# Sums made in place in four tiles of the second feed-forward, and a shorter, reordered opening, in a streaming-encoder layer on one core

## The chip, the core and the metric

The kernel runs on one core of one Trainium2 chip. Times are device microseconds of one launch. The core's engines run side by side and each takes its instructions in the order in which they were written to it: PE does matmuls (PEld is its weight load), ACT (ScalarE) and DVE (VectorE) do elementwise work, POOL does little here, and SP issues most of the DMAs. An engine waits on semaphores for what the others make.

## The reference, cut to what matters

One encoder layer in float32 on 256 tokens of width 2048, with a gated feed-forward (inner width 5632) at its beginning and at its end:

```
x = x + 0.5 * swiglu(rms_norm(x, ffn1_norm), ffn1_w_up, ffn1_w_down)
...                       # gated recurrences, then attention over 256 memory tokens
x = x + 0.5 * swiglu(rms_norm(x, ffn2_norm), ffn2_w_up, ffn2_w_down)
return rms_norm(x, final_norm)

def swiglu(h, w_up, w_down):
    gate, up = split(h @ w_up, 2)
    return (silu(gate) * up) @ w_down
```

The change touches the last feed-forward (ffn2) and the first few microseconds of the first (ffn1).

## The kernel before

**Three products for one.** PE multiplies rounded float32 numbers. Each weight tile of 128 x 2048 is loaded into a buffer called `raw`; ACT makes `h`, its rounded copy, and DVE makes `l` = raw - h. The activations are split in the same way into `xh` and `xl`. A product is then h by xh, h by xl and l by xh. `split` (L155) issues the two instructions of a split: ACT at L156, DVE at L157.

**Kinds of tiles.** `plan_ffn` (L166) lists the weight tiles of a feed-forward and gives each a kind; `prepare` (L278) issues its load, sums and splits; `ffn` (L613) issues its matmuls. A "plain" tile gives eight products. A "fast" tile gives seven products of sums of its quarters (as in Strassen's scheme), and needs a second tile `td` with four such sums, 512 columns each: DVE makes the first two with one instruction (L317), the third at L319 and the fourth at L320. Its own last 1536 columns are split into `h` and `l`, and `td` in two halves of 1024 into `th` and `tl`. A "ready" tile finds its four sums in memory, made and stored earlier in the launch, so that `td` is a load (L309) and not work for DVE.

**The second feed-forward.** It has eleven groups of 512 columns, `wu2[g, p]` with eight tiles p in the order 1, 3, 4, 0, 2, 5, 6, 7, and between the groups tiles of the down projection, `wd2`, which work on the turned results of earlier groups (`hidop`). Which tiles are "ready" is said by `sums_ready` (L88); what is left "fast" is: in group 1 tile 6, in group 2 tile 6, in group 3 tiles 5 and 7, in later groups three or four. Tile p of group g is called "tile g.p" below, and t1_7 is the stored sums of tile 1.7.

**What sets the order.** `weights` (L238) prepares two tiles ahead of the one that PE multiplies. A scheduler lays the instructions of each engine in an order, and the pools set the waits: a load waits until the buffer that it overwrites has had its last reader. In ffn2 `raw_tile` (L261) gives out five buffers of 8 KB a partition in a fixed rotation, three from the pool `raw` and then two from `raw2`; a tile and its `td` take one each. Three `h` buffers hold `h` and `th`. The pool `slots` has 22 buffers of 4 KB a partition. SP issues its loads strictly in its list's order, so a load that waits for its buffer holds back those behind it.

**The opening.** `head_x` (L740) loads the block p of the activations (`xf`), `operand_pairs` (L530) scales it by the norm's gains into `xg` (two ACT instructions at L537) and splits it into `xh` and `xl`. Block 0 is made otherwise (`rounded`, `remainder`, L732 and L735); it is scaled into `xg` only for the sums of activations that later tiles need. Nine matmuls on a tile of ones (L143), two passes each, run on PE before its first product.

Of the kernel before, what the change touches and what calls it, by code (L numbers as in the profile page):

```python
# [10 lines left out]
ACT = mybir.ActivationFunctionType  # L11
ALU = mybir.AluOpType

P = 128
T = 256
# [79 lines left out]
def block_kernel(ctx: ExitStack, tc: tile.TileContext, xT, xin, memT, vec, gfin, bgate, lruw, wu1, wd1, win, wv,  # L95
# [15 lines left out]
    scoped = {}  # L111
# [27 lines left out]
    ones = const.tile([P, P], F32, name="ones")  # L139
    dve.memset(ones, 1.0)  # L140
    warm = bank("warm")
    for _ in range(9):
        pe.matmul(warm[:, :P], ones, ones, start=True, stop=True)  # L143
    eps = const.tile([P, 1], F32, name="eps")
    act.activation(eps, ones[:, :1], ACT.Copy, scale=EPS)
# [20 lines left out]
    def plan_ffn(name, wu, wd):  # L166
        for e in orders[name]:
            src = wd[e[4], e[3]] if e[0] == "down" else wu[e[1], e[2]]
            kind = "fast" if e[0] == "fast" else "added" if name == "ffn1" and e[0] == "mixed" and f"M{e[2]}" in FIRST[e[1]] else "plain"
            if e[0] == "down" and 0 < e[4] < NG - 1 and e[4] % 2 == 0 and e[3] % 2:  # L170
                kind = "added"
            if adds(name, e):
                kind = "fast added"
            if sums_ready(name, e):
                kind = "ready"
                t = kept.tile([P, 2048], F32, name=f"t{e[1]}_{e[2]}")
                made_ahead.append((src, t))
                src = src, t
            plan.append(((name,) + e, src, kind))
# [98 lines left out]
    def prepare(src, kind, cuts=1):  # L278

        if kind == "added":  # L280
            raw, l = begun.pop(0)
            h = hp.tile([P, 2048], F32R, name="h", tag="h")
            done["high"] = act.activation(h, raw, ACT.Copy).ins
            return h, l
        raw = raw_tile()
        n = 2048 // cuts
        if kind == "plain":
            h, l = split_tiles()
            for a in range(0, 2048, n):
                first = opening and len(pairs1) == 1 and cuts > 1  # L290
                quarter = src.rearrange("p (a n) -> (p a) n", n=n)[a // n * P:][:P] if cuts > 1 else src
                sp.dma_start(raw[:, a:a + n], quarter)
                if first and not a:
                    dve.tensor_scalar(out=h[:, :n], in0=raw[:, :n], scalar1=1.0, scalar2=None, op0=ALU.mult)
                    remainder(0)
                    done["low"] = dve.tensor_tensor(out=l[:, :n], in0=raw[:, :n], in1=h[:, :n].bitcast(F32),
                                                    op=ALU.subtract).ins
                else:
                    split(h[:, a:a + n], l[:, a:a + n], raw[:, a:a + n])
                if first and a == n:  # L300
                    sp.dma_start(opening[0][:, 272:], block(272, 256))
                    rounded(1)
                    remainder(1)
            return h, l
        if kind == "ready":
            src, t = src
            sp.dma_start(raw[:, 512:], src[:, 512:])
            td = raw_tile()
            sp.dma_start(td, t)  # L309
        else:  # L310
            sp.dma_start(raw, src)
            if "raw2" in scoped:
                td = raw_tile()
            else:
                td = scoped["wide"].tile([P, 2048], F32, name="td", tag="wide")
            two = [v[:, a:a + 1024].rearrange("p (i n) -> p i n", i=2) for v, a in ((td, 0), (raw, 512))]
            dve.tensor_tensor(out=two[0], in0=raw[:, None, :512].broadcast_to([P, 2, 512]), in1=two[1],  # L317
                              op=ALU.subtract)
            dve.tensor_tensor(out=td[:, 1024:1536], in0=raw[:, 1024:1536], in1=td[:, :512], op=ALU.subtract)  # L319
            dve.tensor_tensor(out=td[:, 1536:], in0=raw[:, 1536:], in1=td[:, 1024:1536], op=ALU.subtract)  # L320
        h, l = split_tiles()
        if kind != "fast added":
            split(h[:, 512:], l[:, 512:], raw[:, 512:])
        else:
            act.activation(l[:, 512:], raw[:, 512:], ACT.Copy, scale=-1.0)
            nc.gpsimd.dma_start(l[:, 512:], src[:, 512:], accum_op=ALU.add)
            done["high"] = act.activation(h[:, 512:], raw[:, 512:], ACT.Copy).ins
        th = hp.tile([P, 2048], F32R, name="h", tag="h")
        if "wide" in scoped:
            tl = scoped["wide"].tile([P, 2048], F32R, name="tl", tag="wide")  # L330
        else:
            tl = lp.tile([P, 2048], F32R, name="tl", tag="l")
        for a in (0, 1024):
            split(th[:, a:a + 1024], tl[:, a:a + 1024], td[:, a:a + 1024])
        return (h, l), (th, tl)

    def product(xs, *ws, late=()):
# [189 lines left out]
    BOTH = [0, 2, 4, 6]  # L527
    xd = []

    def operand_pairs(src, gain, q, xg, out, every=False, made=None):  # L530


        for a in src:
            i = len(out)
            g = xg[:, i * 512:(i + 1) * 512]
            for z in range(2):
                act.activation(g[:, z * T:][:, :T], a[:, z * T:(z + 1) * T], ACT.Copy,  # L537
                               scale=gain(4 * q + 2 * i + z))
            if made:
                h, l = made  # L540
            else:
                h, l = slot(F32R, "xh"), slot(F32R, "xl")
                split(h[:, :512], l[:, :512], g)
            less = None if i else (h[:, 512:768], l[:, 512:768])
            if every:
                less = None
                if q == 3:
                    if not i:
                        xd.append(slot(F32R, "xd"))
                    less = [xd[-1][:, a:a + 256] for a in (512 * i, 512 * i + 256)]  # L550
            elif 2 * q + i in BOTH:
                n = 512 * (BOTH.index(2 * q + i) % 2)
                if not n:
                    xd.append(scoped["xd"].tile([P, 1024], F32R, name="xd", tag="xd"))
                less = [xd[-1][:, a:a + 256] for a in (n, n + 256)]
            out.append(((h, l), less))

        def sums(which=((0, "less"), (0, "sums"), (1, "less"), (1, "sums"))):
            s = slot(name="xs")
            for i, ((h, l), less) in enumerate(out):  # L560
                a = [xg[:, i * 512 + j * P:][:, :P] for j in range(4)]

                def made(h, l, n, at, terms):
                    o = [s[:, at + j * P:][:, :P] for j in range(n)]
                    for j, (x, y, op) in enumerate(terms(o)):
                        dve.tensor_tensor(out=o[j], in0=x, in1=y, op=op)
                    split(h, l, s[:, at:at + n * P])

                if less and (i, "less") in which:
                    made(*less, 2, 0, lambda o: ((a[0], a[1], ALU.subtract), (a[2], a[3], ALU.subtract)))  # L570
                if (every or i or 2 * q in BOTH) and (i, "sums") in which:
                    if not every and not i and len(which) > 1:
                        s = slot(name="xs")
                    made(h[:, 512:], l[:, 512:], 4, 512 * i,
                         lambda o: ((a[1], a[3], ALU.add), (o[0], a[0], ALU.subtract),
                                    (a[1], a[0], ALU.subtract), (a[2], o[1], ALU.subtract)))

        return sums
# [161 lines left out]
    def head_x(p):  # L740

        q = p // 2
        if p % 2 == 0:
            xq[q] = slot(name="xf"), slot(name="xg"), []
        src, xg, out = xq[q]
        a = p % 2 * 512
        if p == 0:
            opening.append(slot(name="xf")[:, :528])
            sp.dma_start(opening[0][:, :272], block(0, 272))
            opening.extend((slot(F32R, "xh"), slot(F32R, "xl")))  # L750
            rounded(0)
            sums = None
            pairs1.append(((opening[1], opening[2]), None))
            return
        sp.dma_start(src[:, a:a + 512], block(16 + p * 512, 512))
        if p == 1:
            operand_pairs([opening[0][:, 16:]], gain1, 0, xg, out, made=opening[1:])
            pairs1[0] = out[-1]
        if p == 6:
            sp.dma_start(vt[:, :small_n], vec[:, :small_n])  # L760
        sums = operand_pairs([src[:, a:a + 512]], gain1, q, xg, out)
        if p % 2:
            sums1.append(sums)
        pairs1.append(out[-1])
# [683 lines left out]
```

## Time and profile before

| | |
|---|---|
| median of three runs | 2412.63 us (2412.18 to 2413.09) |
| the profiled execution | 2412.53 us |
| its span in the profile | 2410.8 us |
| PE busy | 2399.4 us (100%) |
| DVE, ACT busy | 2048.3 us (85%), 1466.6 us (61%) |
| granted TensorE clock | 0.999 |
| second feed-forward | about 1740 us to the end |

The profiled execution is 1.7 us longer than its span and 0.1 us under the median. In the views below a row of the timeline has the start in us, the length in us, the engine, the line, the operation, what it writes and reads, how many such instructions run one behind the other, and in brackets the idle time ahead of it with what ended it.

### The profile page before, as it was taken

Reading aid. Unit: us, or ns where it says so; the run is one execution under the profiler, and the core shown is the slowest. Engines: PE = TensorE matmul, PEld = TensorE weight load, DVE = VectorE, ACT = ScalarE, POOL = GpSimd, SP = SyncE. Lnnn points to the kernel's source line nnn. Section 1 sums busy time; section 2 is a strip of 40 time slices with the busy share of each in tenths; the row PEclk is TensorE's granted clock in tenths of the full one; section 3 lists DMA queues with packets and bytes.
Section 4 is the critical chain, followed back from the end, with each engine's and each line's share of the span. In section 5 each row is a group of like instructions: output and inputs, shape, how many; then the busy total and the mean of one; then the engine's idle time right before and its main releaser. Section 6 shows DMA issues by size and latency. Waiting matters only on the chain.

```text
span 2410.8 us, 30823 instructions
## 1 busy us (share of the span) xinstructions
PE 2399.4 (100%) x12102; PEld 2004.9 (83%) x12102; DVE 2048.3 (85%) x2292; ACT 1466.6 (61%) x1502; POOL 101.3 (4%) x164
## 2 busy tenths in 40 slices
PE   9999999999999999999999999999999999999998
PEld 8888888888888888888888888888888888888887
DVE  7999999999866878679786777777799999999995
ACT  8567777777654454476434555545676666666664
POOL 0000000000000000000000000000000000000000
PEclk9999999999999999999999999999999999999999
DMA  8578999999858776769989899876688877787873
GB/s 316 195 233 255 276 276 278 275 275 273 267 216 303 290 265 264 285 263 342 347 339 336 315 343 338 324 290 234 247 312 323 301 273 284 269 294 273 292 279 145
DMA packets 102098, 681.45 MB, mean 283 GB/s; under 512 B 11328, under 2 KB 11840, under 8 KB 29248
## 3 DMA queue, kind: packets, MB, share of 16 engines
q1 hardware_dynamic: 78912, 519.04, 57.4%
q0 software_dynamic: 23040, 160.44, 22.3%
q8 instruction: 95, 1.56, 0.2%
q14 instruction: 51, 0.42, 0.0%
HBM read 617.57 MB, written 61.87 MB: 282 GB/s over the span
## 4 chain that ended last, share of the span: by engine, by line
PE 97%; DVE 1%; DMA 1%; ACT 1%; issue 0%; SPq 0%; ACTq 0%
PE acc L596 36%; PE acc L598 18%; PE acc L345 11%; PE acc L370 8%; PE acc L371 8%; PE acc L373 8%; PE acc L348 6%; PE acc L636 1%; PE acc L513 1%; DMA raw<-wu 1%; DVE tl L157 0%; DVE l L157 0%; PE acc L962 0%; ACT h L156 0%; PE acc L1261 0%
## 5 line engine op out<-in xcount | busy, mean ns | idle before, releaser
L156 ACT ACTIVATE h<-raw 128x2048 fp32r<-128x2048 f32 (+3 forms) x577 | 868.0, 1528 | 643.6 <-PE acc L371 201.4
L157 DVE TENSOR_TENSOR l<-raw,h 128x2048 fp32r<-128x2048 f32 (+2 forms) x405 | 832.8, 2059 | 233.3 <-ACT h L156 230.4
L596 PE MATMUL acc<-h,xh 128*128 128x512 f32 x1220 | 476.0, 392 | 2.4 <-ACT h L156 2.4
L596 PE MATMUL acc<-h,xl 128*128 128x512 f32 x1220 | 473.6, 390 | 0.0
L596 PE MATMUL acc<-h,hidop 128*128 128x512 f32 x1408 | 352.3, 391 | 0.2 <-ACT h L156 0.2
L370 PE MATMUL acc<-h,ops 128*128 128x512 f32 x832 | 326.8, 393 | 0.0
L371 PE MATMUL acc<-h,ops 128*128 128x512 f32 x832 | 324.6, 390 | 0.0
L596 PEld LDWEIGHTS acc<-h,hidop 128*128 128x128 f32 x1408 | 262.8, 188 | 54.1 <-ACT h L156 0.6
L345 PE MATMUL acc<-ops,h 128*128 128x512 f32 x1152 | 277.6, 393 | 0.0
L596 PEld LDWEIGHTS acc<-h,xh 128*128 128x128 f32 x1220 | 229.1, 188 | 55.5 <-ACT h L156 7.7
L596 PEld LDWEIGHTS acc<-h,xl 128*128 128x128 f32 x1220 | 229.3, 188 | 46.3 <-DVE xl L157 0.2
L345 PEld LDWEIGHTS acc<-ops,h 128*128 128x128 f32 x1152 | 211.6, 188 | 41.1
L157 DVE TENSOR_TENSOR tl<-raw,h 128x1024 fp32r<-128x1024 f32 x172 | 203.4, 1218 | 12.4 <-ACT h L156 11.9
L373 PE MATMUL acc<-l,ops 128*128 128x512 f32 x832 | 206.2, 390 | 0.0
L156 ACT ACTIVATE h<-td 128x1024 fp32r<-128x1024 f32 x140 | 146.6, 1055 | 82.1 <-DVE td L317 31.2
L598 PE MATMUL acc<-l,hidop 128*128 128x512 f32 x704 | 190.9, 390 | 0.0
L370 PEld LDWEIGHTS acc<-h,ops 128*128 128x128 f32 x832 | 156.3, 188 | 32.2
L373 PEld LDWEIGHTS acc<-l,ops 128*128 128x128 f32 x832 | 156.2, 188 | 32.3
L371 PEld LDWEIGHTS acc<-h,ops 128*128 128x128 f32 x832 | 156.5, 188 | 31.2
L598 PE MATMUL acc<-tl,xh 128*128 128x512 f32 x624 | 177.6, 392 | 0.0
L157 DVE TENSOR_TENSOR tl<-td,h 128x1024 fp32r<-128x1024 f32 x140 | 169.8, 1217 | 8.3 <-ACT h L156 7.5
L598 PE MATMUL acc<-l,xh 128*128 128x512 f32 x600 | 165.7, 390 | 0.0
(262 smaller groups left out, 2490.7 us busy)
## 6 DMA issues: line engine op xcount, KB each, us to landing
raw<-wu SPq DMA_DIRECT2D x115, 1024.0 KB, 6.6
raw<-wd SPq DMA_DIRECT2D x88, 1024.0 KB, 6.5
prep<-wu POOLq DMA_DIRECT2D x57, 1024.0 KB, 6.9
t<-prep POOLq DMA_DIRECT2D x57, 1024.0 KB, 6.0
raw<-t SPq DMA_DIRECT2D x57, 1024.0 KB, 6.9
raw<-wu SPq DMA_DIRECT2D x57, 768.0 KB, 4.7
raw<-win SPq DMA_DIRECT2D x40, 1024.0 KB, 5.0
raw<-wg SPq DMA_DIRECT2D x32, 1024.0 KB, 6.0
```

Source lines behind the costliest of these rows:

```text
L156: done["high"] = act.activation(h, raw, ACT.Copy).ins
L157: done["low"] = dve.tensor_tensor(out=l, in0=raw, in1=h.bitcast(F32), op=ALU.subtract).ins
L345: pe.matmul(acc, h[:, k * P:(k + 1) * P], xs[k], start=k == 0, stop=False)
L348: done["product"] = pe.matmul(acc[:, :T], l[:, k * P:(k + 1) * P], xs[k][:, :T], start=False, stop=k == KT - 1).ins
L370: pe.matmul(accs[t], x[:, t * P:][:, :P], h[j], start=first and j == 0, stop=False)
L371: pe.matmul(accs[t], x[:, T + t * P:][:, :P], h[j], start=False, stop=False)
L373: done["product"] = pe.matmul(accs[t], x[:, t * P:][:, :P], l[j], start=False, stop=last and j == 3).ins
L513: pe.transpose(acc[:, z * T + t * P:][:, :P], tile[:, t * 512 + (2 * y + z) * P:][:, :P], ident)
L596: pe.matmul(acc, a, b, start=start, stop=False)
L598: pe.matmul(acc, ah, bl, start=False, stop=stop)
L636: pe.transpose(acc[:, z * T + t * P:][:, :P], hid[t][:, (2 * y + z) * P:][:, :P], ident)
```

## The change

**The four tiles of ffn2.** Fast tiles of groups below 4 get the kind "fast early". Their `td` is a buffer of the pool `slots` with the first two sums only. The third sum overwrites the first 512 columns of `raw`, which nothing reads any more, and the fourth the second 512 columns, after these were split: so L320 is issued behind the split. `th` and `tl` of the second half are made from `raw`. Such a tile takes one buffer of the rotation and not two, and keeps it until its second half is split. The rotation stands one place further after these four tiles in all that follows.

**The opening.** Eight warming matmuls instead of nine. The scaling of block 0 into `xg`, which stood ahead of the scaling of block 1, is issued with block 2, behind its split.

```
-    for _ in range(9):
+    for _ in range(8):
         pe.matmul(warm[:, :P], ones, ones, start=True, stop=True)
...
+            if name == "ffn2" and kind == "fast" and e[1] < 4:
+                kind = "fast early"
             if sums_ready(name, e):
                 kind = "ready"
...
             sp.dma_start(raw, src)
-            if "raw2" in scoped:
+            early = kind == "fast early"
+            if early:
+                td = slot(name="td")
+            elif "raw2" in scoped:
                 td = raw_tile()
...
+            third, fourth = (raw[:, :512], raw[:, 512:1024]) if early else (td[:, 1024:1536], td[:, 1536:])
...
-            dve.tensor_tensor(out=td[:, 1024:1536], in0=raw[:, 1024:1536], in1=td[:, :512], op=ALU.subtract)
-            dve.tensor_tensor(out=td[:, 1536:], in0=raw[:, 1536:], in1=td[:, 1024:1536], op=ALU.subtract)
+            dve.tensor_tensor(out=third, in0=raw[:, 1024:1536], in1=td[:, :512], op=ALU.subtract)
+            if not early:
+                dve.tensor_tensor(out=fourth, in0=raw[:, 1536:], in1=third, op=ALU.subtract)
         h, l = split_tiles()
...
+        halves = [td[:, a:a + 1024] for a in ((0,) if kind == "fast early" else (0, 1024))]
+        if kind == "fast early":
+            dve.tensor_tensor(out=fourth, in0=raw[:, 1536:], in1=third, op=ALU.subtract)
+            halves.append(raw[:, :1024])
...
+    def scaled(g, a, gain, k):
+        for z in range(2):
+            act.activation(g[:, z * T:][:, :T], a[:, z * T:(z + 1) * T], ACT.Copy, scale=gain(k + z))
...
             if made:
                 h, l = made
             else:
+                scaled(g, a, gain, 4 * q + 2 * i)
                 h, l = slot(F32R, "xh"), slot(F32R, "xl")
...
         sums = operand_pairs([src[:, a:a + 512]], gain1, q, xg, out)
+        if p == 2:
+            scaled(xq[0][1], opening[0][:, 16:], gain1, 0)
```

The first place is ACT in the opening, from the last two quarters of the first weight tile on. Before:

```order
L156 ACTIVATE h<-raw 128x512 x2
L537 ACTIVATE xg<-xf 128x256 x4
L156 ACTIVATE xh<-xg 128x512
L156 ACTIVATE h<-raw 128x512 x4
L537 ACTIVATE xg<-xf 128x256 x2
L156 ACTIVATE xh<-xg 128x512
L156 ACTIVATE h<-raw 128x512 x4
L537 ACTIVATE xg<-xf 128x256 x2
L156 ACTIVATE xh<-xg 128x512
```

And with the change:

```order
L156 ACTIVATE h<-raw 128x512 x2
L543 ACTIVATE xg<-xf 128x256 x2
L156 ACTIVATE xh<-xg 128x512
L156 ACTIVATE h<-raw 128x512 x4
L543 ACTIVATE xg<-xf 128x256 x2
L156 ACTIVATE xh<-xg 128x512
L543 ACTIVATE xg<-xf 128x256 x2
L156 ACTIVATE h<-raw 128x512 x4
L543 ACTIVATE xg<-xf 128x256 x2
L156 ACTIVATE xh<-xg 128x512
```

The four scalings (blocks 0 and 1) are two (block 1) now, and the two of block 0 stand between block 2's split and the weight tile that goes with block 2.

The second place is SP at the end of group 1: the load of tile 1.6 (the one at L311, or L313 with the change), and what is issued behind it, with the names' numbers. Before:

```order
L311 DMA raw_14684<-wu2 128x2048
L309 DMA raw_14723<-t1_7_111 128x2048
L307 DMA raw2_14721<-wu2 128x1536
L292 DMA raw_14756<-wd2 128x2048
L292 DMA raw_14797<-wd2 128x2048
```

And with the change:

```order
L313 DMA raw_14683<-wu2 128x2048
L309 DMA raw2_14720<-wu2 128x1536
L311 DMA raw2_14722<-t1_7_110 128x2048
L294 DMA raw_14755<-wd2 128x2048
L294 DMA raw_14796<-wd2 128x2048
```

Tile 1.7 (`wu2 128x1536`) is loaded ahead of its stored sums instead of behind them, and since tile 1.6 takes no second buffer, each of the four loads takes the buffer one place earlier in the rotation. Group 2 ends in the same way.

The third place is ACT at the end of group 5, which stands for groups 4 to 10; here `raw_16401` (before) and `raw_16400` are tile 5.7, `raw_16403` and `raw_16402` are its `td`, and the 128x2048 tiles are two of the down projection. Before:

```order
L156 ACTIVATE h_16407<-raw_16401 128x1536
L156 ACTIVATE h_16411<-raw_16403 128x1024
L156 ACTIVATE h_16439<-raw_16438 128x2048
L156 ACTIVATE h_16411<-raw_16403 128x1024
L683 ACTIVATE hid_16465<-acc_16194 128x512
L156 ACTIVATE h_16480<-raw2_16479 128x2048
```

And with the change:

```order
L156 ACTIVATE h_16406<-raw_16400 128x1536
L156 ACTIVATE h_16410<-raw_16402 128x1024
L156 ACTIVATE h_16438<-raw2_16437 128x2048
L156 ACTIVATE h_16479<-raw2_16478 128x2048
L156 ACTIVATE h_16410<-raw_16402 128x1024
L696 ACTIVATE hid_16464<-acc_16193 128x512
```

Though no operation of these groups is changed, the second half of `th` now stands behind both down tiles on ACT, where it stood between them. DVE's `l` of the second down tile moves ahead of that half's `tl` likewise; PE does five matmuls of the first down tile ahead of this half, where it did three; and SP issues the two down loads in the order in which they are needed, where the second went first.

More of the change, by code (lines that the diff above doesn't have):

```diff
@@ L332, in prepare @@
             tl = lp.tile([P, 2048], F32R, name="tl", tag="l")
-        for a in (0, 1024):
-            split(th[:, a:a + 1024], tl[:, a:a + 1024], td[:, a:a + 1024])
+        for a, t in zip((0, 1024), halves):
+            split(th[:, a:a + 1024], tl[:, a:a + 1024], t)
         return (h, l), (th, tl)
@@ L535, in operand_pairs @@
             g = xg[:, i * 512:(i + 1) * 512]
-            for z in range(2):
-                act.activation(g[:, z * T:][:, :T], a[:, z * T:(z + 1) * T], ACT.Copy,
-                               scale=gain(4 * q + 2 * i + z))
             if made:
```

## The prediction

> **What bounds the kernel now.** I read the page's busy shares and its chain first, then what PE waits for in the second feed-forward, then the timelines around the longest of these waits, and the opening.
>
> ```profile
> span 2410.8 us, 30823 instructions
> PE 2399.4 (100%) x12102; PEld 2004.9 (83%) x12102; DVE 2048.3 (85%) x2292; ACT 1466.6 (61%) x1502; POOL 101.3 (4%) x164
> PE 97%; DVE 1%; DMA 1%; ACT 1%; issue 0%; SPq 0%; ACTq 0%
> PE acc L596 <- ACT h L156: 2.3, 3, 1.2
> ```
>
> PE is the bound, and the change takes one short warming matmul from it and no product. It can only gain where PE waits. The last line is PE's waits from 1740 us on (total, times, longest): three waits for ACT's `h`, 2.3 us in all. That is the prize in the second feed-forward; the rest is what reordering costs.
>
> **Group 1.** PE, ACT, DVE and SP around the first wait, PE around the second, the landing of tile 2.7 (size, us from issue to landing), and DMA traffic in the stretch before (last columns: clock, DMA share, GB/s):
>
> ```profile
> 1800.37 0.39 PE L598 MATMUL acc<-l,xh 128*128 128x512 f32 x1
> 1801.66 0.50 PE L596 MATMUL acc<-h,xh 128*128 128x512 f32 x1 [0.90 <-ACT h L156]
> 1795.32 1.06 ACT L156 ACTIVATE h<-raw 128x1024 fp32r<-128x1024 f32 x1 [0.72 <-DVE raw L317]
> 1799.17 4.33 ACT L156 ACTIVATE h<-raw 128x1536 fp32r<-128x1536 f32 x4 [2.79 <-DMA raw<-wu]
> 1798.53 0.68 DVE L320 TENSOR_TENSOR raw<-raw,raw 128x512 f32<-128x512 f32 x1
> 1784.85 1.75 DVE L157 TENSOR_TENSOR l<-raw,h 128x1536 fp32r<-128x1536 f32 x1
> 1786.52 2.35 DVE L157 TENSOR_TENSOR tl<-raw,h 128x1024 fp32r<-128x1024 f32 x2
> 1790.59 0.33 SPq L309 DMA_DIRECT2D raw<-t  x1
> 1790.96 0.43 SPq L307 DMA_DIRECT2D raw<-wu  x1
> 1790.96 8.11 DMA raw<-wu
> 1851.68 0.61 PE L598 MATMUL acc<-l,xh 128*128 128x512 f32 x2
> 1853.47 0.50 PE L596 MATMUL acc<-h,xh 128*128 128x512 f32 x1 [1.18 <-ACT h L156]
> 1849.37 0.68 DVE L320 TENSOR_TENSOR raw<-raw 128x512 f32<-128x512 f32 x1
> 1842.28 0.42 SPq L307 DMA_DIRECT2D raw<-wu  x1
> raw<-wu SPq DMA_DIRECT2D x1, 768.0 KB, 8.6
> 1780.00:1800.00 20.00, 20.00 (x90) 16.58 (x89) 18.07 (x15) 12.17 (x11) 0.00 (x0) 1.00 0.90 331
> ```
>
> ACT's row of four begins with tile 1.7's `h`, which lands at 1799.07 (1790.96 + 8.11), and only then comes the second half of tile 1.6's `th`. That half's last sum ended at 1799.21 (1798.53 + 0.68), so it could have been done from about 1799.24 to 1800.30 (1.06, as for the first half). Instead it ends 1.33 us later, and PE starts at 1801.66 where 1800.60 was due (1800.37 and one matmul's 0.23, the distance of matmuls in a running row). Lost are 1.06 and 0.11 (the first matmul after a stop takes 0.50 and not 0.39): **1.17 us**. Why it lands late: its load takes a buffer behind the stored sums, which SP issued at 1790.59.
>
> With the change tile 1.7 goes ahead of these sums and takes the buffer that the `l` at 1784.85 leaves at 1786.60; the sums take that of the `tl` pair, free at 1788.87. Issued 4.36 earlier, with the same 8.11 it lands at 1794.7, and ACT has done its `h` while DVE makes the third and fourth sum. Those stay as they were (the same three instructions with the same shapes in the same order on DVE; what they write is another buffer, so I take them at their old lengths, and at 0.1 us more or less for the range). So the half is ready at about 1800.30. PE now does one `l` matmul less ahead of it, and wants it at 1800.37. What is late next is therefore the fourth sum itself, 0.07 us short of costing. I take the whole **-1.17**. The 4 KB buffer of `td` I take as free in time: 22 are in turn, and those of the operands that it follows were last read in earlier stages. No row of before shows such a wait; if the buffer were late, DVE's first sum would be, and the half by as much, up to the loss of the 1.17 and no gain beyond it.
>
> **Group 2** is the same place one group on. Tile 2.7 was issued at 1842.28 and took 8.6, to 1850.88, while the fourth sum ended at 1850.05. PE resumed at 1853.47 where 1852.13 was due: 1.34 and 0.11, **-1.45**. Here the half can be ready at 1851.13 against 1851.68, with 0.5 us to spare; the profile names PE for ACT's idle time there, but the landing is what fits. Group 3 has no such wait, and its loads go out earlier: nothing.
>
> *A rule weighed.* The first term rests on ACT not stepping round a tile that has not landed: the row shows 2.79 us idle and then the tile's `h` first. The Trainium skill, Perfetto Trace Analysis, section on the tensor engine's instruction, says the same: ACT and DVE are strict FIFO. By that rule all of 1.17 is SP's order; with a queue that let the ready half pass, before would have no wait and this term would be nothing.
>
> **Groups 4 to 10** keep their operations, but the rotation shifts, and the order around each group's end with it. Group 5 and group 6 before:
>
> ```profile
> 2030.58 0.86 PE L596 MATMUL acc<-h,hidop 128*128 128x512 f32 x3
> 2031.30 0.50 PE L596 MATMUL acc<-h,xh 128*128 128x512 f32 x1
> 2028.31 0.39 PE L596 MATMUL acc<-h,xl 128*128 128x512 f32 x1
> 2028.39 2.86 ACT L156 ACTIVATE h<-raw 128x2048 fp32r<-128x2048 f32 x2 [2.45 <-DMA raw<-wd]
> 2031.63 1.91 ACT L156 ACTIVATE h<-raw 128x2048 fp32r<-128x2048 f32 x1
> raw<-wd SPq DMA_DIRECT2D x1, 1024.0 KB, 4.9
> raw<-wd SPq DMA_DIRECT2D x1, 1024.0 KB, 6.9
> raw<-wd SPq DMA_DIRECT2D x1, 1024.0 KB, 8.3
> 2091.90 0.96 PE L596 MATMUL acc<-h,hidop 128*128 128x512 f32 x3 [0.19 <-ACT h L156]
> 2082.37 7.45 DMA raw<-wd
> ```
>
> Before, ACT waited until 2028.39 for the down tile that was needed first but loaded second (issue to landing 6.9; its neighbours 4.9 and 8.3). Now that tile is loaded first and the other one second, at the time at which the second load went before: it lands at about 2028.3. Its `h` needs the `h` buffer of tile 5.7, which PE reads last at 2028.31 to 2028.70. So ACT: 2028.70 and 1.91 give about 2030.55 (neighbours overlap by 0.1), and 1.06 for the half: 2031.6. PE wants it after five `hidop` matmuls in place of three: 2030.58 + 5 x 0.23 = 2031.7. It just holds, with 0.1 us. In group 6 the load at 2082.37 landed at 2089.83, PE lost 0.35 + 0.11 + 0.15 + 0.11 there (starts of 2091.90 and of the matmuls behind it against steps of 0.23): 0.7. Now that wait goes, but the half comes at about 2092.7, when PE wants it. Between a gain of 0.7 and, in each of seven groups, a wait of 0.1 with a restart of 0.11 (+1.5) I take **-0.4**, nearer to the gain, since group 5's own rows come out on the good side.
>
> **Opening.** ACT, PE and DVE, and the load of block 1:
>
> ```profile
> 3.54 0.43 SPq L755 DMA_DIRECT2D xf<-xT  x1
> xf<-xT SPq DMA_DIRECT2D x1, 256.0 KB, 5.2
> 8.18 1.69 ACT L537 ACTIVATE xg<-xf 128x256 f32<-128x256 f32 x4
> 10.45 2.18 ACT L156 ACTIVATE h<-raw 128x512 fp32r<-128x512 f32 x4
> 11.12 0.51 PE L596 MATMUL acc<-h,xh 128*128 128x512 f32 x1 [0.29 <-ACT h L156]
> 17.00 0.63 ACT L156 ACTIVATE xh<-xg 128x512 fp32r<-128x512 f32 x1
> 17.67 0.69 DVE L157 TENSOR_TENSOR xl<-xg,xh 128x512 fp32r<-128x512 f32 x1 [0.45 <-ACT xh L156]
> 23.05 0.63 ACT L156 ACTIVATE xh<-xs 128x512 fp32r<-128x512 f32 x1 [1.43 <-DVE xs L566]
> 31.20 1.90 ACT L156 ACTIVATE h<-raw 128x2048 fp32r<-128x2048 f32 x1
> 33.16 0.50 PE L596 MATMUL acc<-h,xh 128*128 128x512 f32 x1
> ```
>
> PE waits at 11.12 for the `h` that stands behind all four scalings. Two of them (0.84) move. But block 1 was issued at 3.54 and took 5.2: it lands at about 8.75, and ACT can't begin its scalings before 8.8. They began at about 9.0 (8.18 and half of 1.69). So only 0.2 of the 0.84 is won: 10.92 for 11.12, **-0.20**. The warming matmul less (two of 18 passes of 0.21, 0.4) adds nothing: the first products can start that much earlier, and PE then waits that much longer for this same `h`. Were this cover gone, it would be another -0.4.
>
> Then the price: block 2's `xh` done, two scalings (0.85) go ahead of block 2's weights and block 3. Block 3's `xh` starts at about 17.65, not 17.00: 0.85 later, less the 0.2 won. DVE waits for just that `xh` (0.45 idle), ACT at 23.05 for DVE's sums (1.43 idle), so the delay travels round; I find no slack in between until ACT's `h` at 31.20, whose end at 33.10 PE takes up at 33.16. Block 4's product can take 0.6 of it unharmed; block 5's starts at about 33.8 for 33.16. Block 6's has 1 us. So PE at block 5 is **0.65 later** than before, which includes the 0.20 won (it is waited away).
>
> **Sum**, against the profiled 2412.53: -1.17 - 1.45 - 0.4 + 0.65 = -2.37, so 2410.2. That execution lies 0.1 under the median of the runs, which changes nothing at this precision.
>
> **Rivals.**
>
> 1. *The opening gains.* For it: the scalings are on PE's path at 11.12, and 0.2 to 0.9 lie there. Against: the 31.20 row, where PE has 0.05 of slack. With -0.3 in place of +0.65, 2410.2 becomes 2409.2; with all of 0.84 won, 2408.7.
>
> 2. *Bandwidth (partly hidden).* The 20 us before the first wait moved 331 GB/s at a share of 0.90. If earlier issue only lengthens the transfers, tile 1.7 still goes ahead of 1 MB of sums in SP's order, which is worth some 2 us of landing (6.4 to 8.1 per load, two on the way); it would have to land after 1798 to cost. Then half of both waits remains: 2411.5. The Trainium skill, DMA: Bandwidth & Descriptors, section Specifications, gives about 358 GB/s of HBM per core as the limit; the trace's 331 lies 8% under it and agrees, so by that page little is gained from issuing earlier, and this rival would be the case, at 2411.5.
>
> 3. *Slower: the end of groups 4 to 10.* The second `th` half now stands behind the second down tile on ACT, and the `l`s on DVE likewise. That tile lands at 2028.3, and ACT takes it up at 2028.7. If it landed as late as the third load did (8.3 in place of 6.9, 1.4 later), the half would be 1.0 us late beyond the 0.4 and 0.1 of margin, PE would stop for that and 0.11, and seven groups would cost 7 to 8 us: 2410.6 without the -0.4, so about 2418. It decides from half a us of lateness of that load on, and passes 0.2% from 1.4 us. For it: the margin is thin everywhere. Against: SP issues in order, and the second load's place in time is unchanged. A mild form, 0.2 a group, gives 2412.0.
>
> 4. *The change doesn't do what it says.* Only four tiles are early; were tile 1.7 and 2.7's buffers not free sooner, only the opening's +0.65 would show: 2413.2. The rows at 1784.85 and 1786.52 speak against it.
>
> **How the numbers follow.** My sum 0.50, opening gains 0.12, bandwidth or mild lateness (2411.5 to 2412) 0.22, nothing but the opening 0.08, seven late groups 0.05, other gains beyond 0.2% 0.03. A measurement of this kernel can tell about 0.2%, 4.8 us, from no change: none but the third rival in full and an unseen gain pass that. The range takes in the first two rivals, the mild form of the third and a tenth or two on each side: 2408.5 to 2412.6.
>
> **What would show it.** PE without a wait at 1800 and 1852, tile 1.7 landing by 1796 and 2.7 by 1848; the first product of block 1 at 10.9 and that of block 5 at 33.8; at group ends PE's step from `hidop` to `h` within 0.1 of 0.23. I am wrong if ACT waits for tile 1.7 as before, if PE's waits for `h` from 1950 on exceed 1 us in all, or if block 5's product comes no later than before.

## The result, and the profile after

The changed kernel takes 2416.36 us (median of 22 runs, 2412.57 to 2418.18) against 2412.53 us (22 runs, 2410.53 to 2415.61): the ratio is 1.0014, with a 95% interval from 1.0008 to 1.0020. It is slower by some 3.5 us (3.8 between the medians), where 2.4 us less were forecast. That is under the 0.2% named in the prediction, and the single runs of the two kernels overlap, but the interval lies above 1. The profiled execution took 2415.37 us, 1.0 under the median, with a span of 2413.5, 2.7 longer than before.

The page's span, PE's busy time and the chain's shares, and PE's waits from 1740 us on (total, times, longest):

```profile
span 2413.5 us, 30820 instructions
PE 2400.3 (99%) x12100; PEld 2002.4 (83%) x12100; DVE 2049.5 (85%) x2292; ACT 1467.7 (61%) x1502; POOL 101.6 (4%) x164
PE 93%; DMA 3%; ACT 2%; DVE 2%; issue 1%; SPq 0%; ACTq 0%; DVEq 0%
PE acc L609 <- ACT h L156: 3.8, 6, 1.1
```

PE is as busy as before, but its share of the chain fell from 97% to 93%, and its waits for `h` went from 2.3 us in three to 3.8 in six. They are not the same waits. Here are SP, ACT, DVE and PE where the first one was, in the order of the forecast's steps:

```profile
1786.61 0.33 SPq L309 DMA_DIRECT2D raw<-wu  x1
1796.75 1.49 ACT L156 ACTIVATE h<-raw 128x1536 fp32r<-128x1536 f32 x1 [0.75 <-PE acc L609]
1798.04 0.68 DVE L337 TENSOR_TENSOR raw<-raw 128x512 f32<-128x512 f32 x1
1798.76 4.78 ACT L156 ACTIVATE h<-raw 128x1024 fp32r<-128x1024 f32 x4 [0.51 <-DVE raw L337]
1800.13 0.39 PE L609 MATMUL acc<-h,xl 128*128 128x512 f32 x1
1800.36 0.39 PE L609 MATMUL acc<-h,xh 128*128 128x512 f32 x1
```

Tile 1.7 is issued at 1786.61 (1790.96 before), its `h` is done by 1798.24, the half that PE waited for is first in ACT's next row, and PE steps by 0.23 where it stood still for 1.06. At 1851 PE stops no more either. That part is as forecast.

The new waits lie in groups 4 to 10. This is group 9, with SP, ACT, DVE and PE around its middle, then PE and ACT at the end of group 6:

```profile
2254.25 0.33 SPq L311 DMA_DIRECT2D raw<-t  x1
2255.39 0.60 SPq L309 DMA_DIRECT2D raw<-wu  x1
raw<-wu SPq DMA_DIRECT2D x1, 768.0 KB, 7.4
2262.09 0.68 DVE L327 TENSOR_TENSOR raw<-raw,raw 128x512 f32<-128x512 f32 x1
2262.86 4.33 ACT L156 ACTIVATE h<-raw 128x1536 fp32r<-128x1536 f32 x4 [2.94 <-DMA raw<-wu]
2263.89 0.39 PE L609 MATMUL acc<-h,xl 128*128 128x512 f32 x1
2265.34 0.50 PE L609 MATMUL acc<-h,xh 128*128 128x512 f32 x1 [1.07 <-ACT h L156]
2090.83 1.07 PE L609 MATMUL acc<-h,hidop 128*128 128x512 f32 x4
2092.41 0.50 PE L609 MATMUL acc<-h,xh 128*128 128x512 f32 x1 [0.52 <-ACT h L156]
2089.49 2.87 ACT L156 ACTIVATE h<-raw 128x2048 fp32r<-128x2048 f32 x2 [1.55 <-DMA raw<-wd]
```

The ACT row at 2262.86 is the row that stood at 1799.17 before, one tile earlier in the group: four splits, 2.9 us idle for a landing, and first in line a tile (9.6) that the ready second half of tile 9.5's sums must let pass. Tile 9.6 is issued behind its 1 MB of sums and lands 7.4 us later; before, in this group, it went first and took 4.2:

```profile
2254.07 0.33 SPq L307 DMA_DIRECT2D raw<-wu  x1
2255.20 0.60 SPq L309 DMA_DIRECT2D raw<-t  x1
raw<-wu SPq DMA_DIRECT2D x1, 768.0 KB, 4.2
```

The two landings that the last views show are group 9's. Over groups 4 to 10 tile 6 took 4.2 to 4.4 us before and 5.6 to 7.4 with the change, and PE waited in the three groups where it took 6.9 or more. Groups 5 and 8 with the change:

```profile
raw<-wu SPq DMA_DIRECT2D x1, 768.0 KB, 5.6
raw<-wu SPq DMA_DIRECT2D x1, 768.0 KB, 6.9
```

In group 9 PE lost 1.22 (2265.34 less 2263.89 and a step of 0.23) and 0.11 for the restart. Counted in this way over the profiled execution, waits in the middle of a group (4, 8, 9) cost 3.0 us, and waits at its end, after the `hidop` matmuls (4, 6, 9, 10), 2.7, where these groups lost 0.8 in all in the profile of before. With 2.6 won in groups 1 and 2 and 0.3 lost in group 3 that is 2.6 us longer; the opening of this execution was 0.15 shorter. It adds up to the span's 2.7 within 0.3.

### The profile page after: what moved, and what is told of

It is laid out like the page before. It is cut to its first block, busy times and chain, and to the rows that moved or that the text cites. A ratio compares the mean times of both kernels' runs of the same rounds, so it can differ in the third digit from the quotient of the medians.

```text
span 2413.5 us, 30820 instructions
## 1 busy us (share of the span) xinstructions
PE 2400.3 (99%) x12100; PEld 2002.4 (83%) x12100; DVE 2049.5 (85%) x2292; ACT 1467.7 (61%) x1502; POOL 101.6 (4%) x164
## 4 chain that ended last, share of the span: by engine, by line
PE 93%; DMA 3%; ACT 2%; DVE 2%; issue 1%; SPq 0%; ACTq 0%; DVEq 0%
PE acc L609 33%; PE acc L611 16%; PE acc L356 11%; PE acc L381 8%; PE acc L382 8%; PE acc L384 8%; PE acc L359 6%; ACT h L156 2%; DMA raw<-wu 1%; DMA raw<-wd 1%; PE acc L649 1%; DVE tl L157 1%; DVE l L157 1%; PE acc L524 1%; PE acc L977 0%
## 5 line engine op out<-in xcount | busy, mean ns | idle before, releaser
L156 ACT ACTIVATE h<-td 128x1024 fp32r<-128x1024 f32 x144 | 150.9, 1055 | 87.2 <-DVE td L323 33.1
L157 DVE TENSOR_TENSOR tl<-td,h 128x1024 fp32r<-128x1024 f32 x144 | 174.7, 1217 | 8.4 <-ACT h L156 7.5
```

Of the source, the lines that this page charges most:

```text
L157: done["low"] = dve.tensor_tensor(out=l, in0=raw, in1=h.bitcast(F32), op=ALU.subtract).ins
```

## The experiments

The first experiments take the change apart and move its side effect into the kernel before.

**The opening alone** (the four tiles as before).

```
-            if name == "ffn2" and kind == "fast" and e[1] < 4:
+            if name == "ffn2" and kind == "fast" and e[1] < 0:
```

> The opening's edits alone (eight warming matmuls, block 0 scaled later); the second feed-forward as before. The theory now: the opening comes out even, because the first block's landing moves with the run; -0.3 to +0.1 us against before (2412.2 to 2412.6), with block 5's first product within 0.2 us of 33.1. The prediction's own step: block 5's product at 33.8 and +0.65 us (2413.2). If the opening is what costs: +2 us or more.

Measured: 2413.23, ratio 1.0002 (0.9993 to 1.0011): not to be told from none. Its profile, ACT's `xh` of block 3 and PE at block 5:

```profile
17.99 0.63 ACT L156 ACTIVATE xh<-xg 128x512 fp32r<-128x512 f32 x1
34.14 0.50 PE L609 MATMUL acc<-h,xh 128*128 128x512 f32 x1 [0.41 <-ACT h L156]
```

Block 5 begins at 34.14, not within 0.2 of 33.1 as this expectation had it: it is the prediction's own step that shows, 0.3 beyond its size. More on it below.

**The four tiles alone** (the opening of before).

```
-    for _ in range(8):
+    for _ in range(9):
...
-                scaled(g, a, gain, 4 * q + 2 * i)      # moved back ahead of "if made:"
-        if p == 2:
-            scaled(xq[0][1], opening[0][:, 16:], gain1, 0)
```

> The four tiles' sums in place alone, with the opening of before. The theory that the shifted rotation costs: about +3.5 us against before (2416), no PE wait at 1800 and 1852, and the new waits in groups 4 to 10, 5 to 7 us in all. The rival that the opening costs: -2.6 us (2409.9).

Measured: 2415.53, ratio 1.0012 (1.0003 to 1.0021). Nearly all of the loss is here. The new waits were expected at 5 to 7 us; its profile, of the shortest of the eleven executions (2413.41), shows 3.7 in groups 4 to 10, and no wait at 1800 or 1852.

**The tiles, with the rotation given back.** Tiles 1.6 and 2.6 only; behind each one place of the rotation is skipped.

```
-            if name == "ffn2" and kind == "fast" and e[1] < 4:
+            if name == "ffn2" and kind == "fast" and e[1] < 3:
...
                 td = slot(name="td")
+                skips.append(1)
...
+        if kind == "plain" and skips:
+            skips.pop()
+            next(loads)
         raw = raw_tile()
```

> The change, but with only tiles 1.6 and 2.6 made in place, and one place of the rotation of raw buffers skipped behind each, at the next tile of the down projection; so the orders of all engines from group 3 on are those of before. The theory that the shifted rotation costs: the gain of 2.6 us in groups 1 and 2 stays and nothing is given back, 2409.5 to 2410.3, no wait of PE for h over 0.2 us at 1800 or 1852 and group 6's 0.7 as before. The rival that in-place sums or their 4 KB buffers cost by themselves (DVE or ACT slower on them): 2413 or more, with longer sums at 1793 to 1800.

Measured: 2411.40, ratio 0.9995 (0.9986 to 1.0004). PE's waits for `h` in ffn2 are 0.2 us in one. So the in-place sums of these two tiles cost nothing that shows. But the time is 1 us above what was expected, and only about 1 us below before, where 2.6 had been priced. Its block 5 began at 33.79, 0.6 later than in the profile of before; the rest is taken up below.

**The shift alone, in the kernel before.**

```
             k, src, kind = plan.pop(0)
+            if k == ("ffn2", "fast", 4, 1):
+                next(loads)
```

> Before, with nothing of the change: one place of the rotation of raw buffers is skipped ahead of the first tile of group 4, so that groups 4 to 10 have the buffers, and the orders, that they have with the change. The theory that the shifted rotation costs: 5 to 6.5 us slower than before, 2417.5 to 2419, with PE waits in the middle and at the end of groups, and the waits of groups 1 and 2 still there. The rival that the four tiles themselves cost: no change, 2412.5.

Measured: 2416.27, ratio 1.0016 (1.0007 to 1.0025). Nothing is made in place, and it loses 4 us, less than the 5 to 6.5 expected. The rotation's place is enough for a loss.

The next experiments ask what of the shift costs: the buffers, or the orders that came with them.

**The loads' order.** In the change, a ready tile's sums always behind the tile. This takes back fourteen pairs in groups 4 to 10, not seven: the change also loads the first tile of each of these groups (tile 1) behind its sums.

```
-            sp.dma_start(raw[:, 512:], src[:, 512:])
+            first = sp.dma_start(raw[:, 512:], src[:, 512:]).ins
             td = raw_tile()
-            sp.dma_start(td, t)
+            with tc.issue_after(first):
+                sp.dma_start(td, t)
```

> The change, with one edit: a ready tile's stored sums are issued by SP behind the tile's own load, never ahead of it. In groups 4 to 10 tile 6 is then loaded ahead of its 1 MB of sums, as before the change; with that the scheduler also puts the second half of tile 7's sums back ahead of the second down tile on ACT. The rotation stays shifted. If the cost is not the buffers but these two orders that came with them: about 5 us faster than the change, 2410 to 2412, no PE wait in the middle of a group and none over 0.3 us at its end. If the shifted buffers themselves come free too late: still 2415 or more.

Measured: 2409.76, ratio 0.9991 (0.9982 to 1.0000): 6.6 us under the change by the two medians, 5.5 by the two ratios, and 2.5 under before. The view of PE's waits from 1740 us on has no row at all. SP and ACT in group 9:

```profile
2252.99 0.33 SPq L309 DMA_DIRECT2D raw<-wu  x1
2253.37 0.42 SPq L312 DMA_DIRECT2D raw<-t  x1
2258.11 1.50 ACT L156 ACTIVATE h<-raw 128x1536 fp32r<-128x1536 f32 x1 [0.59 <-PE acc L610]
2260.41 4.34 ACT L156 ACTIVATE h<-raw 128x1024 fp32r<-128x1024 f32 x4 [0.80 <-DVE raw L328]
```

The tile is split at 2258.11, while DVE is still at the third sum (the fourth begins at 2259.69), and ACT's next row begins with the half that PE wants, released by that sum and by no landing. The shifted buffers stay: they were not what cost. The edit alone doesn't tell the loads' order from ACT's, since with it the scheduler also put the second half back ahead of the second down tile.

**The order of splits at the end of groups.** In the change, a down tile is split only behind the second half of the last sums.

```
+                elif "hid" in scoped:
+                    with tc.issue_after(done["high"]):
+                        split(h[:, a:a + n], l[:, a:a + n], raw[:, a:a + n])
```

> The change, with one edit: each tile of the down projection in the second feed-forward is split on ACT and DVE only behind the second half of the last sums before it. Only the order at the end of groups is taken back; tile 6 of groups 4 to 10 is still loaded behind its sums. If both orders cost: the waits at the ends of groups go (2 to 3 us), those in their middle stay (about 3 us); 2413 to 2414. If the loads are the whole cost: no gain, 2416.

Measured: 2416.09, ratio 1.0015 (1.0006 to 1.0024), no gain. PE's waits from 1740 us on, and ACT and PE at one of them, in group 9:

```profile
PE acc L612 <- ACT h L156: 3.1, 5, 1.1
2264.56 4.33 ACT L156 ACTIVATE h<-raw 128x1536 fp32r<-128x1536 f32 x4 [2.42 <-DMA raw<-wu]
2267.05 0.50 PE L612 MATMUL acc<-h,xh 128*128 128x512 f32 x1 [0.55 <-ACT h L156]
```

No wait at a group's end is left in its trace; five groups now wait in the middle, 4.4 us in all, where three did for 3.0. That PE only reaches the next late tile earlier fits this, but isn't shown. The edit also loads the first tile of each group ahead of its sums again; what is left of the new orders is tile 6 behind its sums, and the loss is as large. So the end's order, which the prediction had as its slower rival, is not what costs by itself.

**Both orders.** Both edits above.

> The change with both edits, the loads' order and the splits' order. It should come out with the loads' order alone, 2410 to 2412, if that already brings the second back; less only if a wait at the ends of groups is left there.

Measured: 2409.45, ratio 0.9989 (0.9980 to 0.9998), as with the loads' order alone.

**The rotation given back, with the opening of before.** The edits of both earlier runs.

> Tiles 1.6 and 2.6 made in place, the rotation given back behind each, and the opening of before: what the runs point to as the fastest. Against the same with the new opening (2411.4 median) it should be 0.5 to 0.7 us faster if the opening's delay of block 5 is real, so 2410.6 to 2410.9, and 1.5 to 2 us under before; equal or slower if the opening's edits are worth nothing or a gain.

Measured: 2410.57, ratio 0.9996 (0.9987 to 1.0004): as expected, though 0.8 us between two medians of this spread decides nothing.

The next experiments go at two of the prediction's own grounds: why groups 1 and 2 waited, and the opening.

**The loads' order in the kernel before.** The edit of the loads' order, and nothing of the change.

> Before, with one edit and nothing of the change: a ready tile's stored sums are issued behind the tile's own load. On SP only two pairs change places, the loads of tiles 1.7 and 2.7 with their sums. If the waits of groups 1 and 2 were SP's order and not a lack of buffers, both go without any sum made in place: about 2.5 us faster than before, 2409.7. If tile 1.7 and 2.7 need the buffer that the change frees: no change, 2412.3.

Measured: 2413.70, ratio 1.0007 (0.9998 to 1.0016). A miss in the time, not in the place. PE at 1800 and at the end of group 3:

```profile
1800.28 0.39 PE L597 MATMUL acc<-h,xl 128*128 128x512 f32 x1
1800.66 0.50 PE L597 MATMUL acc<-h,xh 128*128 128x512 f32 x1
1908.30 1.42 PE L597 MATMUL acc<-h,hidop 128*128 128x512 f32 x5 [1.55 <-ACT h L156]
1905.85 0.60 ACT L684 ACTIVATE hid<-acc 128x512 f32<-128x512 f32 x1 [2.11 <-PE acc L599]
```

Two swapped pairs on SP took the wait at 1800 from 1.17 to 0.27, and there is none at 1851. But the scheduler also put group 3's copy of an accumulator (L684) ahead of a down tile's `h` on ACT, and PE lost 1.8 there, and 1.5 at group 6, 0.8 more than before, for the down tile that lands second. Whether it would gain with ACT's old order was not tried.

**The opening's two edits, one at a time**, on the change with the loads' order: the whole old opening, then eight warming matmuls with the scalings where they were, then nine with the scalings moved.

```
-    for _ in range(8):
+    for _ in range(9):                                  # first and third
...
-        if p == 2:
-            scaled(xq[0][1], opening[0][:, 16:], gain1, 0)   # first and second
```

> The change's four tiles with the loads' order, and the whole opening of before. By the opening's delay of block 5 (33.0 to 34.1 us with the new opening, 32.9 to 33.9 with the old) 0.3 to 0.6 us faster than the same with the new opening, so 2409.1 to 2409.5; equal if that delay is only the landing's luck.

> As the one before, with eight warming matmuls and the first scalings where they were. A warming matmul less should be worth nothing: PE waits that much longer for block 1's h. Block 5's first product at 32.9 to 33.4, time as with the old opening.

> As before it, with nine warming matmuls and the first scalings moved behind block 2's split. If the delay comes from the moved scalings: a stop of 0.5 us ahead of block 5's first product, and 0.3 to 0.6 us more than with the old opening.

Measured: 2409.88, 2410.73 and 2410.38 (ratios 0.9990, 0.9992 and 0.9992, each within 0.0009), beside 2409.76 with the new opening. The gain of 0.3 to 0.6 us that was expected of the old opening doesn't show: the times tell nothing apart. In the profiles PE stops for 0.58 ahead of block 5 in the third and for 0.12 to 0.14 in the first two.

One question was left: whether the pair of loads costs without the shifted rotation.

**Tile 6 behind its sums, in the kernel before.**

```
+            if late:                                     # group above 3, tile 6
+                td = raw_tile()
+                sums_in = sp.dma_start(td, t).ins
+                with tc.issue_after(sums_in):
+                    sp.dma_start(raw[:, 512:], src[:, 512:])
```

> Before, with before's rotation and buffers; only in groups 4 to 10 tile 6 is issued behind its 1 MB of stored sums, as it is with the change. ACT's order is that of before. If that pair's order is what the change gives its gain away to: 3 to 5 us slower than before, 2415.5 to 2417.5, with PE waits ahead of the second half of tile 5's sums in the middle of groups. If it costs only together with the shifted buffers: no change, 2412.4.

Measured: 2416.30, ratio 1.0015 (1.0006 to 1.0024), 3.9 us slower, in the range expected. ACT and PE in group 9, and the waits:

```profile
2266.34 4.33 ACT L156 ACTIVATE h<-raw 128x1536 fp32r<-128x1536 f32 x4 [2.98 <-DMA raw<-wu]
2268.83 0.50 PE L602 MATMUL acc<-h,xh 128*128 128x512 f32 x1 [1.10 <-ACT h L156]
PE acc L602 <- ACT h L156: 4.9, 6, 1.6
```

ACT's order is that of before, and the rotation too; on DVE and PE the scheduler moved a few steps with the pair. Seven swapped pairs of loads, and what follows from them, make a loss of the change's size, with the change's rows. The profile is of the longest of its eleven executions (2418.41), so its 4.9 us of waits are not the average.

The profiles of five kernels have tile 6 behind its sums in groups 4 to 10: the change, the four tiles alone, the shift, the splits' order and this one. In these 35 places the tile took 6.6 us or more 18 times, and PE waited each time; 17 times it took 6.4 or less, and PE lost at most 0.2.

## Why the prediction was wrong

**Groups 1 and 2, -2.62: the mechanism right, step by step, the size that of one execution.** Tile 1.7's earlier issue, its `h` under DVE's sums, the half ready just before PE wants it, and no wait at 1800 or 1851. The bandwidth rival did not come (tile 1.7 took 7.7 us for 8.1), and the slot that `td` was taken to find free was free. That tile 1.7's place behind its sums was the cause is shown from the other side by the swap in the kernel before.

Group 2's 1.45, though, came from a landing that was late in the profile of before. Three more profiles leave these groups as before: the opening alone, the shift, and tile 6 behind its sums. Here is tile 2.7's landing in them, where the prediction's row has 8.6:

```profile
raw<-wu SPq DMA_DIRECT2D x1, 768.0 KB, 6.4
raw<-wu SPq DMA_DIRECT2D x1, 768.0 KB, 6.5
raw<-wu SPq DMA_DIRECT2D x1, 768.0 KB, 6.2
```

None of the three has a wait there; in group 1 they lost 0.9, 1.4 and 1.0. The mean over the four profiles is 1.5 us in both groups together, not 2.6. That fits the rotation given back, which gains about 1, and the swap in the kernel before: some 1.3 won against 2.6 lost elsewhere in its profile, where the medians lie 1.1 us apart.

**Groups 4 to 10, -0.4: the step that failed.** They cost about 5 us more than before in the two profiles. The step read only the groups' ends, where an order on ACT had visibly moved, and took everything else there as unchanged. In the middle of these groups the shifted rotation gave the sums of tile 6 a buffer that comes free ahead of the tile's own, and SP issued them first. It is the very mechanism that the prediction had just read at 1790.59 and 1790.96 and priced at 1.17: the tile behind 1 MB of sums, its `h` first in ACT's line, the ready half behind it. The change took that pattern out of two groups and put it into seven. In group 9 the landing grows from 4.2 to 7.4 us. The Trainium skill, DMA: Bandwidth & Descriptors, section on queues, rings and completion order, has each DMA engine take a ring's descriptors in order; the two landings agree: the sums issued first landed at 2259.07, the tile at 2262.76.

**The slower rival: the right groups, the wrong place.** It named the second down tile at the groups' ends, at 1 us in all seven. Such waits came (four, 2.7 us), but taking their order back alone gained nothing that could be measured. It had a chance of 0.05; the right mechanism had none. One of the prediction's signs of being wrong was exceeded here: PE's waits for `h` from 1950 on were 3.8 us, against its limit of 1.

**The opening, +0.65: right in kind, its size not settled.** The stop ahead of block 5 is in every profile with the moved scalings (0.53 to 0.58 us in seven) and is 0.12 to 0.15 in the others. But block 5's first product came at 33.01 to 34.14 with them (mean 33.66) and at 32.85 to 33.87 without (eight profiles, mean 33.31): 0.35 later, less than twice the standard error of that difference (0.19), with landings that differ by 1 us from run to run. The times don't show it either. In the changed kernel's own profile block 1 landed early and hid it, so that block 5 came no later than before, another of the prediction's signs of being wrong:

```profile
8.02 0.91 ACT L543 ACTIVATE xg<-xf 128x256 f32<-128x256 f32 x2 [0.41 <-DMA xf<-xT]
33.01 0.50 PE L609 MATMUL acc<-h,xh 128*128 128x512 f32 x1 [0.39 <-ACT h L156]
```

ACT began the scalings at 8.02, not 8.8. That a warming matmul less gains nothing fits the runs, but their times can't show it.

## What to carry to other kernels

Where buffers go round in a fixed rotation, an edit that takes one place less moves every load behind it, and the orders that a scheduler makes of them: compare the whole order of every queue to the end of the program, not only the places edited. Look first for the pattern whose price you have just read, and give each new instance that price. And pin the order that matters: one line that keeps a tile ahead of its sums was worth some 6 us here, and made of the change a version 2.5 us faster than before (2409.76 against 2412.27).

## What the runs showed of the hardware that was not expected

Slack is small against the landings' scatter. Tile 2.7, issued in the same order and 0.4 us behind the same sums, took 8.6, 6.4, 6.5 and 6.2 us in four profiles, and only the first made PE wait. The wait for tile 6 came in three to five of the seven groups, not always in the same ones, as its landing took more or less than about 6.5 us. And a wait taken away need not be time won: with the ends of groups put right, 2.7 us of waits went there, 1.4 came in the middle of groups, and the time stayed. One profiled execution gives the mechanism and the price in that execution, not the average.
